# Moving the final wait on the output store from SP to ACT in a sum of absolute differences

## Chip, cores, metric

One core of a Trainium2 chip. The metric is device microseconds of one execution; where several were run, the median of the fast runs. Engine names: DVE is VectorE, ACT ScalarE, POOL GpSimd, PE TensorE, SP SyncE; a "q" behind a name (SPq) means that the engine's sequencer handled the instruction alone; rows of PE's sequencer are printed as PEldq. A store has landed when its semaphore is complete; a wait retires when it is satisfied and done. A "row" is a line of the profile. Times with two decimals that the views round to 0.1 are read from the packed trace.

## The reference

```python
x, y: (1024, 4096) float32        # random
def reference(x, y, axis):        # axis = -1
    return np.sum(np.abs(x - y), axis=axis).astype(np.float32)   # (1024,)
```

## The kernel before

Each of 128 partitions holds 8 rows (K = 8). DVE subtracts, ACT takes the absolute value and sums along the row with its accumulator. The last row comes in five pieces; the last of these is summed on DVE. The instructions are put straight into the program's main block. After it the framework appends its own end: a barrier of all five engines, a clearing of semaphores by POOL, and a second barrier. `at_end` places one more instruction behind those barriers.

```python
    def at_end(self, emit):
        ...
        def closing(ins):
            if done or nc.cur_bb.bb.name == here or ins.engine != mybir.EngineType.Pool:
                return
            mine = [x.opcode for x in nc.cur_bb.bb.instructions if x.engine == mybir.EngineType.SP]
            if mine.count("EventSemaphore") < 2:      # SP has both of its barrier waits
                return
            done.append(ins)
            emit()
...
            put(lambda: nc.vector.wait_ge(s_end, n_part + 2))
            put(lambda: nc.vector.reduce_sum(out=ro[:, K - 1:K], in_=last, axis=AX, apply_absolute_value=True).then_inc(s_end, 1))
...
    put(lambda: nc.sync.wait_ge(s_end, n_part + 3))
    put(lambda: nc.sync.dma_start(out=orr, in_=ro).then_inc(s_out, 16))      # the store, 4 KB
    entry.at_end(lambda: nc.sync.wait_ge(s_out, 16).then_inc(s_out, -16))    # its wait
```

Of the kernel before, what the change touches and what calls it, by code (L numbers as in the profile page):

```python
# [18 lines left out]
class Entry:  # L19
# [5 lines left out]
    def put(self, emit, before="UnconditionalBranch"):  # L25
        nc = self.nc
        hook = nc.inst_callbacks[-1]
        lower = nc._always_lower_symbolic_ap
        nc.remove_inst_callback(hook)
        nc._always_lower_symbolic_ap = False  # L30
        here = nc.cur_bb.bb.instructions
        n = len(here)
        try:
            emit()
        finally:
            nc._always_lower_symbolic_ap = lower
            nc.push_inst_callback(hook)
        here = nc.cur_bb.bb.instructions
        main = nc.main_func.blocks[0].instructions
        while len(here) > n:  # L40
            mine = here.pop(n)
            first = next(i for i, x in enumerate(main) if x.engine == mine.engine and x.opcode == before)
            main.insert(first, mine)

    def at_end(self, emit):

        nc = self.nc
        hook = nc.inst_callbacks[-1]
        here = nc.cur_bb.bb.name
        done = []  # L50

        def closing(ins):
            if done or nc.cur_bb.bb.name == here or ins.engine != mybir.EngineType.Pool:
                return
            mine = [x.opcode for x in nc.cur_bb.bb.instructions if x.engine == mybir.EngineType.SP]
            if mine.count("EventSemaphore") < 2:
                return
            done.append(ins)
            emit()

        nc.remove_inst_callback(hook)
        nc.push_inst_callback(closing)
        nc.push_inst_callback(hook)
# [3 lines left out]
def kernel(ctx, tc, x, y, axis, out):  # L67
    nc = tc.nc
# [10 lines left out]
    entry = Entry(nc)  # L79
# [23 lines left out]
    s_out = nc.alloc_semaphore("s_out")  # L103
# [62 lines left out]

    put(lambda: nc.sync.wait_ge(s_end, n_part + 3))
    put(lambda: nc.sync.dma_start(out=orr, in_=ro).then_inc(s_out, 16))
    entry.at_end(lambda: nc.sync.wait_ge(s_out, 16).then_inc(s_out, -16))


# [33 lines left out]
```

## Time and profile before

| | before |
|---|---|
| time, median of 3 (range) | 84.38 us (84.36 to 84.47) |
| span of the profiled execution, first to last instruction | 82.8 us |
| time of that same execution | 84.41 us |
| last reduction ends, store issued | 81.31, 81.34 |
| store landed, its wait starts and ends | 82.78, 82.80, 82.82 |
| second closing barrier left by all | 82.6 |

The span is what the trace shows; the time is what is scored. 1.6 us of the time lie outside the span. The lines behind the table are quoted in the prediction (its 82.74 for the landing adds a 1.4 that the view had rounded; the trace has 1.445). The rows by line give operation, count, then the shortest, median and longest duration in ns, then the first and last start. One row was not quoted there, and also belongs here. It is POOL's in the group of the closing barriers, in the view of line 200 (operation, count, then the shortest, median and longest duration in ns, then the first and last start):

```profile
L200 POOLq EVENT_SEMAPHORE  x4: 17/17/17, 82.0 to 82.5; - x4
```

POOL gathers and releases both barriers: in the trace its second release begins at 82.52, and the four others leave between 82.56 and 82.57. So its last instruction, the second release, is the earliest end of any engine: 82.5.

### The profile page before, as it was taken

How to read it: one execution, taken by the hardware profiler on the slowest of the kernel's cores; microseconds unless marked ns; L12 is line 12 of the kernel's file. 1: busy time of each engine (PE TensorE's matmuls, PEld its weight loads, DVE VectorE, ACT ScalarE, POOL GpSimd, SP SyncE). 2: the span in 40 equal slices, each digit the busy share in tenths (PEclk: the TensorE clock that was granted, in tenths of full speed). 3: DMA queues.
4: the chain of work that ended last, by engine and by line, in shares of the span. 5: the costliest groups of instructions: out<-in, count | busy, mean ns of one | idle time of the engine just before them, and what ended most of it. 6: DMA issues, size and time to landing. Idle time of an engine off the chain costs nothing.

```text
span 82.8 us, 104 instructions
## 1 busy us (share of the span) xinstructions
DVE 36.4 (44%) x16; ACT 31.5 (38%) x27; POOL 0.2 (0%) x4
## 2 busy tenths in 40 slices
DVE  0000000000000000000199999999279898999772
ACT  2400000000000000000000988979690599999990
POOL 0000000000000000000000000000000000000000
DMA  5992999989999999998888999859999999999950
GB/s 127 404 807 103 538 538 435 451 388 451 435 451 435 419 467 419 404 451 380 380 380 380 451 617 451 380 253 404 475 388 467 419 404 406 427 413 412 401 195 2
DMA packets 2592, 33.56 MB, mean 405 GB/s; under 512 B 416, under 2 KB 928, under 8 KB 1696
## 3 DMA queue, kind: packets, MB, share of 16 engines
q1 hardware_dynamic: 2448, 25.17, 72.3%
q10 hardware_dynamic: 144, 8.39, 23.4%
HBM read 33.55 MB, written 0.00 MB: 405 GB/s over the span
## 4 chain that ended last, share of the span: by engine, by line
DMA 63%; DVE 22%; SPq 10%; issue 1%
DMA yb_rows<-in_y_dram 63%; DVE xa_rows L128 21%; SPq L116 6%; SPq L119 4%; DVE last_piece L162 1%; DVE ro_sums L164 1%
## 5 line engine op out<-in xcount | busy, mean ns | idle before, releaser
L128 DVE TENSOR_TENSOR xa_rows<-xa_rows,yb_rows 128x4096 f32<-128x4096 f32 x4 | 17.4, 4420 | 41.1 <-DMA yb_rows<-in_y_dram 41.1
L133 ACT ACTIVATE xa_rows<-xa_rows 128x4096 f32<-128x4096 f32 x4 | 14.5, 3617 | 44.5 <-DVE xa_rows L128 44.5
L128 DVE TENSOR_TENSOR xb_rows<-xb_rows,yb_rows 128x2048 f32<-128x2048 f32 (+5 forms) x9 | 17.9, 2015 | 3.5 <-DMA yb_rows<-in_y_dram 3.5
L133 ACT ACTIVATE xb_rows<-xb_rows 128x2048 f32<-128x2048 f32 (+5 forms) x9 | 15.1, 1681 | 3.0 <-DVE xb_rows L128 2.9
L133 ACT ACT_TABLE_LOAD x1 | 1.3, 1283 | 1.7 <-PEq L186 1.7
L133 ACT ACTIVATION_READ_ACCUMULATOR xb_rows<-xb_rows 128x1 f32 x9 | 1.7, 186 | 0.0
L133 ACT ACTIVATION_READ_ACCUMULATOR xa_rows<-xa_rows 128x1 f32 x4 | 0.7, 186 | 0.0
L162 DVE TENSOR_TENSOR last_piece<-xb_rows,yb_rows 128x320 f32<-128x320 f32 x1 | 0.5, 492 | 0.3 <-DMA yb_rows<-in_y_dram 0.3
L164 DVE TENSOR_REDUCE ro_sums<-last_piece 128x1 f32<-128x324 f32 x1 | 0.5, 491 | 0.0
L156 DVE TENSOR_REDUCE ro_sums<-half_sums 128x2 f32<-128x4 f32 x1 | 0.1, 150 | 0.0
L186 POOL MEMSET const-bfloat16-1.0<- 128x1 bf16 x1 | 0.1, 101 | 0.0
L186 POOL MEMSET const-uint8-127<- 128x1 uint8 x1 | 0.1, 101 | 0.0
L186 POOL MEMSET const-float32-0.0<- 128x1 f32 x1 | 0.1, 98 | 0.2 <-issue 0.2
L186 POOL MEMSET const-float32-1.0<- 128x1 f32 x1 | 0.1, 98 | 0.0
## 6 DMA issues: line engine op xcount, KB each, us to landing
xa_rows<-in_x_dram SPq DMA_DIRECT2D x1, 6144.0 KB, 36.9
xb_rows<-in_x_dram SPq DMA_DIRECT2D x1, 6144.0 KB, 54.4
yb_rows<-in_y_dram SPq DMA_DIRECT2D x3, 2048.0 KB, 15.4
xa_rows<-in_x_dram SPq DMA_DIRECT2D x1, 2048.0 KB, 17.0
xb_rows<-in_x_dram SPq DMA_DIRECT2D x1, 864.0 KB, 17.7
yb_rows<-in_y_dram SPq DMA_DIRECT2D x1, 864.0 KB, 15.8
xb_rows<-in_x_dram SPq DMA_DIRECT2D x1, 512.0 KB, 16.6
yb_rows<-in_y_dram SPq DMA_DIRECT2D x1, 512.0 KB, 17.4
```

Of the source, the lines that this page charges most:

```text
L116: put(lambda: nc.sync.dma_start(out=xb[:, H - 1, c], in_=xr[:, K - 1, c]).then_inc(s_piece[i], 16))
L119: put(lambda: nc.sync.dma_start(out=yb[:, H - 1, c], in_=yr[:, K - 1, c]).then_inc(s_piece[i], 16))
L128: put(lambda: nc.vector.tensor_sub(out=tx, in0=tx, in1=ty).then_inc(s_sub, 1))
L133: put(lambda: nc.scalar.activation(tx, tx, ABS, accum_out=to).then_inc(sem, 1))
L156: put(lambda: nc.vector.reduce_sum(out=ro[:, K - 3:K - 1], in_=half, axis=AX).then_inc(s_end, 1))
L162: put(lambda: nc.vector.tensor_sub(out=last[:, n_part:n_part + w], in0=tx, in1=ty).then_inc(s_end, 1))
L164: put(lambda: nc.vector.reduce_sum(out=ro[:, K - 1:K], in_=last, axis=AX, apply_absolute_value=True).then_inc(s_end, 1))
L186: nc = _bacc.Bacc("TRN2", target_bir_lowering=False, num_devices=1)
```

## The change

The intent is to let the store's wait stand on an engine other than the one that issued the store. The wait is the last instruction of ACT, the store stays on SP's queue.

```diff
-            mine = [x.opcode for x in nc.cur_bb.bb.instructions if x.engine == mybir.EngineType.SP]
+            mine = [x.opcode for x in nc.cur_bb.bb.instructions if x.engine == mybir.EngineType.Activation]
...
-    entry.at_end(lambda: nc.sync.wait_ge(s_out, 16).then_inc(s_out, -16))
+    entry.at_end(lambda: nc.scalar.wait_ge(s_out, 16).then_inc(s_out, -16))
```

## The prediction

The Trainium skill's page "Runtime: NRT & Kernel Launch", section "The ~15µs preamble/postamble breakdown", describes a barrier that is passed through the engines and back (a serpentine, 8 hops of 44 ns) in its row of the barrier ahead of the kernel, not of the one behind it. The estimate of 4 hops that the prediction builds on this stays its own guess.

> **What bounds the kernel now.** I read the page first, then the chain that ended last, then the timeline of the last microseconds, then the rows of the three lines that make up the end (the store, its wait, the closing barriers), and last SP's own waits. The page says that the kernel is a load of two inputs with arithmetic beside it:
>
> ```profile
> DVE 36.4 (44%) x16; ACT 31.5 (38%) x27; POOL 0.2 (0%) x4
> ...
> DMA  5992999989999999998888999859999999999950
> ...
> HBM read 33.55 MB, written 0.00 MB: 405 GB/s over the span
> ```
>
> The reader is to see that the DMA row stands at 8 or 9 in nearly every slice while no compute engine is busy for half of the span. ACT, which gets the wait, has no shortage of time, but neither does SP, which loses it. So load on an engine is not what this change is about. What it can touch is the tail, after the last input byte. The end of the chain that ended last, and the timeline of the tail (start, duration, engine), show how short that is:
>
> ```profile
> 67.57 12.70 DMA yb_rows<-in_y_dram
> 80.27 0.02 issue
> 80.29 0.50 DVE last_piece L162
> 80.80 0.02 issue
> 80.82 0.49 DVE ro_sums L164
> ```
>
> ```profile
> 80.06 0.51 ACT L133 ACTIVATE xb_rows<-xb_rows 128x384 f32<-128x384 f32 x1
> ...
> 80.48 0.19 ACT L133 ACTIVATION_READ_ACCUMULATOR xb_rows<-xb_rows 128x1 f32 x1
> 80.82 0.49 DVE L164 TENSOR_REDUCE ro_sums<-last_piece 128x1 f32<-128x324 f32 x1
> 81.34 0.35 SPq L168 DMA_DIRECT2D out_dram<-ro_sums  x1
> ```
>
> The last data arrive at 80.27, the last sum is done at 80.82 + 0.49 = 81.31, and SP issues the store at 81.34. ACT's own last work ended at 80.48 + 0.19 = 80.67. The chain view stops at the reduction; what follows it is only in the rows by line. The rows of the store, of the wait that the change moves (line 169), and of the barriers that the framework puts at the end (all under line 200) are:
>
> ```profile
> L168 SPq DMA_DIRECT2D out_dram<-ro_sums x1: 348/348/348, 81.3 to 81.3; - x1
> ...
> DMA to landing us min/median/max: 1.4/1.4/1.4
> ```
>
> ```profile
> L169 SPq EVENT_SEMAPHORE  x1: 17/17/17, 82.8 to 82.8; - x1
> ```
>
> ```profile
> L200 SPq EVENT_SEMAPHORE  x2: 17/17/17, 82.1 to 82.6; - x2
> L200 ACTq EVENT_SEMAPHORE  x2: 17/17/17, 82.1 to 82.6; - x2
> L200 DVEq EVENT_SEMAPHORE  x2: 21/21/21, 82.1 to 82.6; - x2
> ```
>
> Two things run side by side after 81.34. One is the store: 81.34 + 1.4 = 82.74 until it lands, and the wait retires at 82.8, the end of the span. The other is two barriers of all five engines, of which every engine leaves the second at 82.6. SP then stands in the wait until 82.8, and its own waits give the length:
>
> ```profile
> SPq L169 <- SPq L169: 0.2, 1, 0.2
> ```
>
> So of the store's 1.4 us all but 0.2 us is already hidden behind the barriers. The span is bound by DMA until 80.27 and by a chain of one subtraction, one reduction and one store after it, and the wait on the store is the last thing in it on whatever engine it stands.
>
> **What the Trainium skill says.** "Perfetto Trace Analysis", section "Per-engine timelines" (sequencer-only instructions), says that the profiler reports only the execution of such an instruction, not the time it waited, nor the propagation of the semaphore. The trace agrees: line 169 is 17 ns long although it waited 0.2 us, which is why I take the cost of the wait from its start and from the view of waits. The same page, under the HWDGE timeline, says that the data movement lies outside the issuing instruction and that its semaphore waits for the write to be confirmed, "a surprisingly long delay especially when the write target is HBM"; here the instruction is 0.35 us and the landing 1.4 us. "Trainium Architecture — The Big Picture", section "Inside one NeuronCore", says that each engine has its own instruction stream and that they synchronize only through semaphores: an engine that did not issue the store can wait on its semaphore like any other. "Runtime: NRT & Kernel Launch", section "The ~15µs preamble/postamble breakdown", says that after the kernel the runtime runs a barrier over the five engines, a reset of semaphores and a rearming of the DMA rings, and describes the barrier as a serpentine of 8 hops at 44 ns. No view here shows it: the trace ends at 82.8, while the time of the same profiled execution is 84.41, so 84.41 - 82.8 = 1.6 us lie outside the span, before it or after it.
>
> **The change part by part.** It is one instruction that changes its engine. In the built programs the two lists of instructions are otherwise identical, in order as well: the semaphore wait of the store, with the same semaphore, the same value 16 and the same decrement, is at the same place in the list, behind the second closing barrier, and says ACT where it said SP.
>
> - Removed from SP: one wait of 17 ns, with 0.2 us of standing in front of it. SP is then done when it leaves the second barrier, 82.6 + 0.02 = 82.6, some 0.2 us earlier than now. Nothing inside the kernel uses SP after that. Gain inside the span: 0.
> - Added to ACT: the same wait. ACT leaves the second barrier at 82.6 like SP, which is before 82.8, so the wait is armed 0.2 us before the store's semaphore is complete. It retires when SP's would: 82.8. Cost inside the span: 0, give or take how much faster one sequencer sees a semaphore than the other. For that there is a sample at the start: after the opening barrier SP and ACT each issue a load, and the timeline has both at 1.26. The difference is therefore about 0.01 us.
> - Moved: nothing else. The store stays on SP's queue and still starts at 81.34, since what it waits for, the last reduction, is untouched. ACT's 13 activations stay ahead of the wait in its stream, and the barriers stay ahead of it too, so the wait cannot hold any of them back.
> - Sum inside the span: 82.8 + 0 = 82.8 us. Sum with what lies outside: 84.38 + 0 = 84.38 us.
>
> What remains is the part outside the span. If the runtime's barrier there is passed from engine to engine, the place in the order of the engine that arrives last counts. The four others arrive 0.2 us ahead and have their hops behind them, as far as the late engine lets them. An estimate from the skill's figure: moving the late arrival from the turning point of the serpentine to its beginning would add 4 hops of 44 ns, 0.18 us; moving it the other way would save as much. That is 0.2% of 84.4, and I don't know its sign.
>
> **The rivals.** First, *SP's end is the costly one*: if SP has more to do after the program than the others, or comes late in the closing order, its being free 0.2 us earlier is worth up to 0.2 us, so 84.2. For it: SP is the last engine to finish now. Against it: the end has to collect all engines, and ACT is now as late as SP was. Second, *ACT's end is the costly one*: by the hop estimate 84.38 + 0.18 = 84.56, and if ACT's own closing work is also longer, perhaps 84.7. For it: nothing in the trace but the fact that the 1.6 us are unseen. Against it: ACT's waits in line 200 take the same 17 ns as SP's. Third, *the wait could be lost*, the kernel ending before the store has landed: this would save the 0.2 us. The wait is still there with its value of 16, so no. Fourth, *the wait holds ACT back earlier*, if it stood in front of the activations or a barrier: each barrier would then start after the landing, about 0.5 us per barrier (82.1 to 82.6) or 1 us for both, 85.4. The built order excludes it.
>
> **Range and chances.** To gain or lose 2% takes 1.69 us. The wait is worth 0.2 us, the unseen engine order about as much, and even the whole of what lies outside the span is only 1.6 us. The three runs before lie within 84.36 to 84.47. I take 84.38 as the centre, about 0.2 us down for an order that favours ACT, and a little over 0.2 us up for one that doesn't or for another chip: 84.2 to 84.6. Within 2% has 98 in 100, and the two sides one each for what I haven't thought of.
>
> **What would show it right or wrong.** In the profile of the changed kernel the line 169 row should be ACT's, 17 ns, at 82.8; SP's last row should be the barrier's at 82.6; the wait should be 0.2 us; the store should still land in 1.4 us from 81.3; the span should be 82.8 give or take the DMA's own variation. If the span stays and the time moves by 0.1 to 0.2 us, the order of the engines at the end did it. The prediction is wrong if the wait of ACT begins before the second barrier, if the store is issued or lands at another time, or if the difference between time and span, 1.6 us now, changes by over 0.3 us.

## The result

The changed kernel took 84.41 us (84.29 to 84.73, 6 runs) against 84.42 (84.33 to 84.58, 6 runs) before: ratio 1.000, 95% interval 0.998 to 1.002.

The profile of the changed kernel: first the row of the wait, then the rows of the barriers, then the store.

```profile
L169 ACTq EVENT_SEMAPHORE  x1: 17/17/17, 82.9 to 82.9; - x1
```

```profile
L200 POOLq EVENT_SEMAPHORE  x4: 17/17/17, 82.0 to 82.6; - x4
...
L200 SPq EVENT_SEMAPHORE  x2: 17/17/17, 82.1 to 82.6; - x2
L200 ACTq EVENT_SEMAPHORE  x2: 17/17/17, 82.1 to 82.6; - x2
```

```profile
L168 SPq DMA_DIRECT2D out_dram<-ro_sums x1: 348/348/348, 81.4 to 81.4; - x1
...
DMA to landing us min/median/max: 1.5/1.5/1.5
```

The wait is now ACT's, as long as it was, and retires with the landing. The landing's 1.5 against 1.4 us is rounding: 1.451 and 1.445 in the traces. The span is 82.9 instead of 82.8, and the end of the chain shows that this 0.05 us was there before the change could act: the last load landed at 80.32 instead of 80.27.

```profile
67.63 12.69 DMA yb_rows<-in_y_dram
80.32 0.02 issue
80.34 0.50 DVE last_piece L162
80.84 0.02 issue
80.87 0.49 DVE ro_sums L164
```

So far everything is as predicted. But "same" alone doesn't say why: both engines could be equally good at the end of the critical path, or the wait could have been off that path on both. The experiments ask that.

### The profile page after: what moved, and what is told of

It is laid out like the page before. It is cut to its first block, busy times and chain, and to the rows that moved or that the text cites. A ratio compares the mean times of both kernels' runs of the same rounds, so it can differ in the third digit from the quotient of the medians.

```text
span 82.9 us, 104 instructions
## 1 busy us (share of the span) xinstructions
DVE 36.4 (44%) x16; ACT 31.6 (38%) x27; POOL 0.2 (0%) x4
## 4 chain that ended last, share of the span: by engine, by line
DMA 63%; DVE 22%; SPq 11%; issue 1%
DMA yb_rows<-in_y_dram 63%; DVE xa_rows L128 21%; SPq L116 6%; SPq L119 4%; DVE last_piece L162 1%; DVE ro_sums L164 1%
```

## The experiments

Twelve kernels, on three chips (0, 4 and 12), each beside runs of the kernel before on the same chip. The eight on chip 0 were expected with two theories. Theory 1: the wait is armed before the store lands and what follows does not care which engine is last. Theory 2: what follows the span depends on which engine is last; its sizes, up to 0.18 us, are the prediction's estimate.

### The change again

No edit.

> The changed kernel once more, beside the kernel before on one chip. Theory 1 (the wait is armed before the store lands, so its engine does not matter, and the closing outside the span does not care either): ratio 1.000 within 0.002, time minus span of the profiled execution 1.55 to 1.62 us as in the two profiles so far (1.59 and 1.58). Theory 2 (the order of engines in the closing counts): a steady difference of 0.1 to 0.2 us in the time, and in time minus span, by which the ratio would be outside 0.998 to 1.002.

Measured: 84.39 us (84.23 to 84.50) against 84.38; ratio 0.9994 (0.9982 to 1.0006). Time minus span in the profiled execution: 84.50 - 82.92 = 1.58. The result stands.

### The wait on the three other engines

```diff
 e2   entry.at_end(lambda: nc.vector.wait_ge(s_out, 16).then_inc(s_out, -16))     # and DVE in closing
 e3   entry.at_end(lambda: nc.tensor.wait_ge(s_out, 16).then_inc(s_out, -16))     # and PE in closing
 e4   nc.gpsimd.wait_ge(s_out, 16).then_inc(s_out, -16)     # behind everything, after the kernel's body; at_end's line removed
```

> The same wait, last on VectorE. Theory 1: span 82.8 give or take 0.2, time minus span 1.55 to 1.62 us, ratio to before within 0.998 to 1.002. Theory 2: time minus span differs from SP's and ACT's by [...]up to 0.18.

> The same wait, last on TensorE, whose semaphore instructions took 51 ns in the closing barriers against 17 of SP and ACT. Theory 1: span longer by that 0.03 us at most, time minus span 1.55 to 1.62 us. Theory 2: time minus span differs from SP's by 0.04 to 0.18 us; together with the other engines' it gives the order.

> The same wait, last on GpSimd, behind its release of the second barrier (placed by the launching code, since it has to stand behind everything else of that engine). Theory 1: span 82.8 give or take 0.2, time minus span 1.55 to 1.62 us. Theory 2: as for the others, a shift of 0.04 to 0.18 us in time minus span.

| wait on | time (range), before 84.38 | ratio (95%) | time - span, profiled |
|---|---|---|---|
| DVE | 84.41 (84.36 to 85.08) | 1.0016 (0.9991 to 1.0040) | 1.57 |
| PE | 84.52 (84.49 to 84.62) | 1.0014 (1.0002 to 1.0026) | 1.67 |
| POOL | 84.65 (84.64 to 84.91) | 1.0035 (1.0023 to 1.0047) | 1.88 |

The row of the wait on PE:

```profile
L169 PEldq EVENT_SEMAPHORE  x1: 51/51/51, 82.8 to 82.8; - x1
```

The spans are all 82.8, so by the span these kernels are equal. Outside it they are not: PE costs 0.1 us more and POOL 0.3. This contradicts theory 1, which had a constant 1.6 outside the span, and looks at first like theory 2, though POOL's 0.29 (1.88 against 1.59) is above the 0.18 that theory 2 expected. The rows of the kernel with the wait on POOL give the hint, the barriers first and then the wait:

```profile
L203 POOLq EVENT_SEMAPHORE  x4: 17/17/17, 81.9 to 82.5; - x4
...
L203 SPq EVENT_SEMAPHORE  x2: 17/17/17, 82.0 to 82.5; - x2
```

```profile
L205 POOLq EVENT_SEMAPHORE  x1: 17/17/17, 82.7 to 82.7; - x1
```

POOL's last instruction moved from 82.47, its release in this run, to 82.76, by 0.29 us, while the other engines ended with the barrier; and the time rose by 0.3. On POOL the wait has its whole price; on SP, ACT and DVE it had none that could be seen.

### The wait ahead of the barriers

```diff
 e5   put(lambda: nc.scalar.wait_ge(s_out, 16).then_inc(s_out, -16))      # at_end's line removed
 e6   put(lambda: nc.sync.wait_ge(s_out, 16).then_inc(s_out, -16))
```

> The wait stays on ACT but stands ahead of the two closing barriers instead of behind them. Theory 1 (the place counts, not the engine): ACT reaches the first barrier at 82.8 instead of 80.7, so both barriers run after the landing. In the profile before, SP arrived at the first barrier at 81.9 and all left the second at 82.6, so 0.65 us of barriers and some 0.1 us for ACT's own drain come after 82.8: span 83.4 to 83.7, time 85.0 to 85.3, ratio about 1.009. A theory in which the wait costs the same wherever it stands expects 84.4.

> The same early place, on SP, which also has its drain of 0.12 us between the wait and the barrier. Theory 1: within 0.2 us of the early wait on ACT, so 85.0 to 85.4. If the engine matters in this place, where the rest of the program does depend on it, the two differ by more than 0.2 us.

Measured: 85.40 us (85.38 to 85.45) on ACT, ratio 1.0115 (1.0100 to 1.0130); 85.48 (85.37 to 85.76) on SP, ratio 1.0130 (1.0115 to 1.0146); before 84.41. The place costs 1 us, more than the expected 0.6 to 0.9, and the engine nothing that the intervals separate. The rows of the early wait on ACT show the place:

```profile
L200 POOLq EVENT_SEMAPHORE  x4: 17/17/17, 83.0 to 83.6; - x4
```

```profile
L169 ACTq EVENT_SEMAPHORE  x1: 17/17/17, 82.9 to 82.9; - x1
```

Both barriers now run behind the landing. The expectation fell short because it added 1.6 us to the span; time minus span was 1.79 in both.

### The magnifier: one engine late by 1.7 us

A second, identical store behind the barriers, so that the last engine ends 1.7 us behind the second barrier instead of 0.2. Its last wait is on ACT in one kernel and on SP in its twin.

```diff
-    entry.at_end(lambda: nc.scalar.wait_ge(s_out, 16).then_inc(s_out, -16))
+    def late():
+        nc.sync.wait_ge(s_out, 16)
+        nc.sync.dma_start(out=orr, in_=ro).then_inc(s_out, 16)
+        nc.scalar.wait_ge(s_out, 32).then_inc(s_out, -32)       # twin: nc.sync, and SP in closing
+    entry.at_end(late)
```

> A magnifier: behind the barriers SP waits for the store, stores the same sums a second time, and ACT waits for that. ACT is then the last engine by about 1.5 us instead of 0.2, and SP has ended with the issue. Theory 1: span 82.8 + 1.4 to 1.6 = 84.2 to 84.4, time 85.8 to 86.1, equal within 0.1 us to the twin with the last wait on SP; time minus span 1.55 to 1.62. If an engine that is free early starts a closing of its own that is worth time, time minus span is shorter here than in the twin by what SP gains, up to 1 us.

> The twin of the magnifier: second store as there, and the last wait on SP, so that ACT is free 1.7 us early and SP is last. Theory 1: same time as the twin within 0.1 us, time minus span 1.55 to 1.62. The rival of a costly end of SP: slower than the twin by 0.2 us or more.

Measured: last on ACT 85.81 us (85.78 to 85.81), ratio 1.0163 (1.0150 to 1.0177); last on SP 85.58 (85.56 to 85.63), ratio 1.0139 (1.0125 to 1.0152). The rows of the last waits, ACT's and then the twin's:

```profile
L172 ACTq EVENT_SEMAPHORE  x1: 17/17/17, 84.3 to 84.3; - x1
```

```profile
L172 SPq EVENT_SEMAPHORE  x1: 17/17/17, 84.3 to 84.3; - x1
```

The spans are 84.32 and 84.27, which is 0.05 us of the difference, most of it from the loads (the last one landed at 80.30 and 80.27); time minus span is 1.49 and 1.32. So the engine does matter, by 0.17 us, once it is late enough, and in the opposite sense to the rival in the expectation: it is the late SP that is the cheaper. Theory 1 falls in its constant closing. Theory 2 is right that the engines' closings differ (a closing is here the time from an engine's last instruction to the end of the measured time), but doesn't say why the change itself showed nothing.

**Theory 3.** The time is the latest of five sums: the end of an engine's last instruction plus a closing of that engine's own. The closings follow from the runs in which one engine was clearly last: SP 1.32, ACT 1.49, PE 1.67 us, each from one profiled execution. POOL's comes from the kernel in which its end alone was moved: 84.64 - 82.76 = 1.88. For DVE there is only a bound, 1.57, since it was last in the span but need not have set the time. The table holds the profiled executions against this, with POOL's closing at 1.87, the mean of its ten rows marked *. Ends are start plus duration of each engine's last instruction in the trace.

| kernel | POOL ends | time - POOL's end | last engine: end + its closing | time |
|---|---|---|---|---|
| before | 82.54 | 1.88 * | SP 82.82 + 1.32 = 84.14 | 84.41 |
| changed | 82.58 | 1.87 * | ACT 82.87 + 1.49 = 84.37 | 84.45 |
| changed, again | 82.62 | 1.88 * | ACT 82.92 + 1.49 = 84.41 | 84.50 |
| wait on DVE | 82.50 | 1.87 * | DVE 82.80 + at most 1.57 | 84.37 |
| wait on POOL | 82.76 | 1.88 * | is POOL | 84.64 |
| early, ACT | 83.58 | 1.87 * | PE 83.66 + 1.67 = 85.33 | 85.45 |
| early, SP | 83.63 | 1.87 * | PE 83.71 + 1.67 = 85.38 | 85.50 |
| store on ACT (below) | 82.39 | 1.87 * | ACT 82.73 + 1.49 = 84.23 | 84.26 |
| relay (below) | 82.50 | 1.88 * | ACT 82.81 + 1.49 = 84.31 | 84.37 |
| seven early (below) | 82.31 | 1.88 * | ACT 82.44 + 1.49 = 83.94 | 84.19 |
| wait on PE | 82.49 | 2.00 | PE, gives 1.67 | 84.49 |
| late ACT | 82.57 | 3.24 | ACT, gives 1.49 | 85.81 |
| late SP | 82.53 | 3.06 | SP, gives 1.32 | 85.59 |

In the ten rows with a star the last engine's sum is below the time wherever it is known, and the time follows POOL's end within 0.01 us. In the other three it is the late engine.

The constant alone does not name POOL: in nine of the ten rows the barrier releases all engines at fixed distances from POOL's end, so the time follows, say, DVE's leaving of the barrier as closely. That it is POOL rests on two things. Where POOL's end alone was moved, the time stayed 1.88 behind it, while the time's distance from the ends of the four others grew by 0.3. And the others' closings are too short: in the kernel before DVE left at 82.59, which with at most 1.57 makes 84.16, and PE at 82.62, which with 1.67 makes 84.29, against 84.41.

So in the kernel before, SP's wait had 84.41 - 84.14 = 0.27 us to spare, and in the changed kernel ACT's had 84.45 - 84.37 = 0.08. **The wait was off the path that sets the time on both engines.** The change used up most of the slack and showed nothing.

### Three more ends

Store and wait both on ACT:

```diff
-    put(lambda: nc.sync.wait_ge(s_end, n_part + 3))
-    put(lambda: nc.sync.dma_start(out=orr, in_=ro).then_inc(s_out, 16))
+    put(lambda: nc.scalar.wait_ge(s_end, n_part + 3))
+    put(lambda: nc.scalar.dma_start(out=orr, in_=ro).then_inc(s_out, 16))
```

> Store and wait both on ACT, so that SP has nothing to do at the end. ACT ended its last activation at 80.7, before the last reduction at 81.3, so it issues the store at the same time as SP did, with an issue of 0.37 us (ACT's load) against 0.35. If the landing is 1.4 to 1.5 us as on SP's queue: span 82.8 give or take 0.2, ratio within 0.998 to 1.002. If ACT's queue has a slower start, the landing from issue is over 1.6 us and the time up by as much.

Measured: 84.38 us (84.26 to 84.46) against 84.41; ratio 0.9994 (0.9978 to 1.0011). The landing took 1.5 us. No difference from before that these runs can see.

A relay, in which SP waits for the store and ACT for SP:

```diff
-    entry.at_end(lambda: nc.scalar.wait_ge(s_out, 16).then_inc(s_out, -16))
+    def relay():
+        nc.sync.wait_ge(s_out, 16).then_inc(s_out, 1)
+        nc.scalar.wait_ge(s_out, 17).then_inc(s_out, -17)
...
+    entry.at_end(relay)
```

> Both engines wait, one after the other: SP waits for the store and raises the semaphore by one, ACT waits for that. It costs one passing of a semaphore between two engines at the very end. From the barrier, where GpSimd's raise at 82.5 released the others at 82.6, about 0.05 us: span 82.8 to 83.0, ratio 1.000 to 1.002. Being free early is worth nothing to SP here, so if it was worth something in the change, this is slower than the change by more than that one passing.

Measured: 84.40 us (84.32 to 85.11) against 84.41; ratio 1.0008 (0.9980 to 1.0035). ACT retired 0.04 us behind SP, and that did not show in the time either: by the table ACT had 0.06 us left.

Seven of eight columns stored early, the last never (wrong):

```diff
...
-    put(lambda: nc.sync.wait_ge(s_end, n_part + 3))
-    put(lambda: nc.sync.dma_start(out=orr, in_=ro).then_inc(s_out, 16))
+    put(lambda: nc.sync.wait_ge(s_seven, 1))          # raised by the reduction that completes column 7
+    put(lambda: nc.sync.dma_start(out=orr[:, 0:K - 1], in_=ro[:, 0:K - 1]).then_inc(s_out, 16))
```

> Wrong on purpose: only seven of the eight columns of sums are stored, as soon as the seventh is done (about 78.2), and the last is never stored. The store has then landed before the last reduction ends at 81.3, and the wait on ACT finds it done. Theory 1: the end is then set by the two barriers behind VectorE's last reduction, 81.3 + 0.1 + 0.65 = about 82.0 to 82.1; the span falls by 0.7 to 0.8 us, time 83.6 to 83.7. That is the whole of what the store costs at the end, and the most that any treatment of it could give. If the store were hidden altogether, the time would stay at 84.4.

Measured: 84.13 us (83.83 to 84.19) against 84.41, ratio 0.9955 (0.9933 to 0.9976). The expected 83.6 to 83.7 was missed, for two reasons. The closing is POOL's, 1.88 behind its end at 82.31, and not 1.6 behind the span's. And the end of the chain in this kernel shows that the last load came later than before, at 80.61 instead of 80.27:

```profile
67.62 12.99 DMA yb_rows<-in_y_dram
80.61 0.02 issue
80.63 0.50 DVE last_piece L163
```

The small store lay in the midst of the loads (it took 2.5 us to land), which is the likely cause, but no run separates that from the other differences of this kernel.

### A version that follows from theory 3

If POOL's end sets the time, the barriers have to come earlier, and the wait belongs on the engine with the shortest closing, SP. In the kernel before, the barriers are held by SP, which arrives only after it has issued the store (81.9). Here SP arrives first and issues the store afterwards, while the barriers go on; the store's semaphore is one that POOL's clearing leaves alone (the clearing ran at 81.7, behind the increment by the last reduction, and the wait for 17 was still satisfied at 82.8).

```diff
...            # at_arrival is new; closing now counts 3 of SP's semaphore waits instead of 2
-            ... reduce_sum(out=ro[:, K - 1:K], ...).then_inc(s_end, 1))
+            ... reduce_sum(out=ro[:, K - 1:K], ...).then_inc(s_out, 1))
-    put(lambda: nc.sync.wait_ge(s_end, n_part + 3))
-    put(lambda: nc.sync.dma_start(out=orr, in_=ro).then_inc(s_out, 16))
-    entry.at_end(lambda: nc.sync.wait_ge(s_out, 16).then_inc(s_out, -16))
+    def store():
+        nc.sync.wait_ge(s_out, 1)
+        nc.sync.dma_start(out=orr, in_=ro).then_inc(s_out, 16)
+    entry.at_arrival(store)       # ahead of SP's wait in the first closing barrier, behind its arrival
+    entry.at_end(lambda: nc.sync.wait_ge(s_out, 17).then_inc(s_out, -17))
```

> Correct result wanted. The wait is back on SP, last, and the store is issued behind SP's arrival at the first closing barrier instead of ahead of it, so the barriers no longer stand behind the issue. Theory 3, read from the runs so far: the time is the latest of four sums, the end of each engine's last instruction plus a closing of its own: GpSimd 1.87 us, TensorE 1.67, ACT 1.49, SP 1.32. In the kernel before GpSimd sets it (82.54 + 1.87 = 84.41), and SP's wait has 0.27 us to spare. Here the first barrier can go when VectorE has drained (81.36 instead of SP at 81.93), so GpSimd should end at 82.0 to 82.1 instead of 82.54 (sum 83.9), and SP, whose wait retires with the landing at 82.8 as before, sets the time: 82.82 + 1.32 = 84.14, ratio about 0.997, with time minus span down from 1.59 to 1.32. Theory 1 in its old form (the span sets the time and the closing is a constant 1.6 us whatever the engine): span 82.8 as before, time 84.4.

Measured: correct; 84.15 us (84.02 to 84.36, 6 runs) against 84.42 (84.32 to 84.49, 11 runs), ratio 0.9968 (0.9955 to 0.9981). The rows of this kernel: POOL and the barriers, SP's wait, the store.

```profile
L221 POOLq EVENT_SEMAPHORE  x4: 17/17/17, 81.4 to 82.0; - x4
...
L221 SPq EVENT_SEMAPHORE  x2: 17/17/17, 81.8 to 82.0; - x2
```

```profile
L190 SPq EVENT_SEMAPHORE  x1: 17/17/17, 82.8 to 82.8; - x1
```

```profile
L187 SPq DMA_DIRECT2D out_dram<-ro_sums x1: 348/348/348, 81.4 to 81.4; - x1
```

The store is issued as before and its wait retires at 82.8 as before; the span is 82.84, even a little longer. Only the barriers moved, POOL's end from 82.54 to 82.01. The median time fell by 0.27 us; the profiled execution took 84.16, which is 82.84 + 1.32: SP sets it, as theory 3 said before the run. It is the fastest correct kernel, by 0.3%. That the wait's engine would matter here (ACT's closing would add 0.17 us) is an estimate from the two closings and was not run.

## Why the prediction was right

Its number was right (84.38 predicted, 84.41 measured, range 84.2 to 84.6), and so was the statement that nothing else moves: engine, place, duration of the wait, start of the store and landing were as said, all within the 0.05 us by which the last load came later. Step by step:

- **"Removed from SP ... Gain inside the span: 0", "Added to ACT ... Cost inside the span: 0"**: shown. ACT's wait was armed in time and retired with the landing.
- **"the wait on the store is the last thing in it on whatever engine it stands"**: true of the span, and wrongly read as true of the time. The last instruction of the span did not set the time; POOL's, 0.28 us earlier, did (82.54 against 82.82).
- **"The wait is worth 0.2 us"**, and the third rival with it (losing the wait "would save the 0.2 us"): wrong. In the kernel before, SP's wait had 0.27 us to spare, so by the sums removing it would save nothing. This was not run: the program would no longer wait for its result.
- **The unseen closing, estimated at up to 0.18 us between engines**: that the size fits ACT and SP is luck, as it came from hops that the page gives for another barrier; between SP and POOL it is 0.55. ACT's closing is 1.49 against SP's 1.32, 0.17 more. So the first rival (SP's end is the costly one) is refuted, SP's being the shortest measured, and the second (ACT's end is) has the right sign. It did not show, since POOL's sum is later than both, and not because the end "has to collect all engines" alike.
- **The fourth rival's size, 85.4 us for a wait ahead of the barriers**: measured 85.40 on ACT, but by two errors that cancel. It counted 1 us for both barriers behind the landing, hence a span of 83.8, and 1.6 us outside it. Measured: the barriers took 0.62 us from ACT's arrival at 82.96 to POOL's end at 83.58, the span was 83.66, and 1.79 us lay outside.

The prediction thus reached its number by a sound bound (the change can't touch more than some tenths of a microsecond) and a path that named the wrong last instruction. What stays open: what the closings consist of, which no trace shows; DVE's closing; and whether ACT's and PE's values, each from one kernel on chip 0, hold elsewhere. POOL's was the same in the rows from chips 0 and 4, and SP's in the kernels from chips 0 and 12.

## What to carry to other kernels

The last instruction of a trace need not be the one that sets the time: move the end of one engine at a time, and compare the time with every engine's end. The one that the time keeps following is the one that sets it. A wait at the end belongs on the engine with the most slack behind it, here SP, and what deserves work is whatever delays the engine that is last in that sense, here the barriers that stood behind the issue of the store. An equal time after a move shows only that the slack was enough: here it went from 0.27 to 0.08 us.

## What the Trainium skill lacked or had wrong

- "Runtime: NRT & Kernel Launch", section "The ~15µs preamble/postamble breakdown": lists the stages behind a kernel, but not that an engine's late end costs differently by engine. Measured here, from an engine's last instruction to the end of the time, with whatever of the time lies ahead of the span included: SP 1.32 us, ACT 1.49, PE 1.67, POOL 1.87. Why they lie 0.17 to 0.20 us apart is not shown here.
- "DMA: Bandwidth & Descriptors", section "Anatomy of one DMA — SWDGE (gpsimd) path": gives a fixed cost of about 2.0 us for one transfer on GpSimd's path. It has no such total for SP's and ACT's path, but the skill does: "SBUF — State Buffer", section "The DMA setup-cost knee", puts about 2 us on every transfer. Measured here on that path, this 4 KB store took 1.4 to 1.5 us from issue to landing when it was alone, and one of 3.5 KB took 2.5 us amid the loads.
- No page says that the framework's closing barriers (0.6 us from SP's arrival at 81.9 to the release of the second at 82.5) lie on the path of the time while a store's wait behind them may not.
